# Sixteen of the first layer's 24 stored tiles keep two short first steps, the last eight take one long first step

## The chip, the core and the metric

The program runs on one core of a Trainium2 chip. The engines that matter here are PE (TensorE, matrix products), DVE (VectorE), ACT (ScalarE) and SP, whose queue issues the loads from memory. The metric is the device time of one execution in microseconds (us).

## What is computed

One block of a network over 256 tokens and 2048 features, in float32. A vector `c` gives nine modulation vectors of 2048; then come a gated feed-forward layer, a mixer and a second feed-forward layer. The change lies in the first feed-forward layer.

```python
mod = (jax.nn.silu(c) @ w_ada[l] + b_ada[l]).reshape(B, N_SUBLAYERS, N_MOD, D_MODEL)
def swiglu(h, w_gate, w_up, w_down):
    return (jax.nn.silu(h @ w_gate) * (h @ w_up)) @ w_down
h = modulate(rms_norm(x, gain_pre), shift, scale)     # shift, scale: two of the nine
y = rms_norm(fn(h), gain_post)
return x + weight * (1 + gate[:, None, :]) * y
```

`w_gate` and `w_up` are 2048 x 5632, `w_ada` is 2048 x 18432.

## The kernel before, in words

The 2048 features are 16 blocks of 128. `h` can be made for a feature block only when its columns of `w_ada` (all 2048 rows of them) have been read and summed. So the layer begins by rounds over feature blocks, FIRST_BLOCKS (line 27): round 0 takes blocks 0 and 1, round 1 blocks 2 and 3, and rounds 2, 3 and 4 four blocks each. While one round multiplies, the columns of `w_ada` for a later one are read.

Method `outer` (line 667) runs the rounds. At the start of one, `block` makes `h` for its blocks (`hT` in the rows): products of `x` with a diagonal (`mm<-scale,x`), two ACT passes and one DVE subtraction per block. Then the round goes through 14 loads, numbered 0 to 13 here, gate and up in turn. A load is 512 columns of a weight matrix, that is four tiles of 128 columns, over the feature blocks of the round: 512 KB for two blocks, 1 MB for four. For each two blocks of it, ACT rounds the weights to `hi` (line 186), DVE takes the rest as `lo` (line 187), and PE runs 24 products of 128x256 (line 202: for each tile and block hi with both halves of `h`, then lo with the first).

Loads 0 and 1 keep their sums in PSUM over all rounds. Loads 2 to 13 cannot: these are the 24 stored tiles (FF_SPILL1; a tile is 128 columns of both gate and up). Their products of one step are taken out of two PSUM banks into SBUF tiles `act`: the first step is copied by ACT (line 704), every later one is added by DVE (line 706). MERGES1 (line 28) says at the end of which round a stored load makes a step and from which block: in the first layer at the end of every round. MERGES2, for the second layer, leaves out the end of round 0 and lets the step after round 1 take blocks 0 to 3 in one go.

After each load's issue, `tick` (line 1471) advances the sums over `w_ada` by a number of ticks that RATES (line 30) sets by round: 1.0 per load in round 0, 1.25 in rounds 1 to 3. A tick (`ada_long`) issues one 512 KB piece of `w_ada` (two DMAs of 256 KB) and lets DVE multiply and add the piece of three ticks before (lines 277 and 279: two operations 512 wide for the pieces of round 1, one 1024 wide for later ones). The modulation for round 1 takes 14 ticks: eight pieces, three ticks of lag, three of hold; the last step are products with ones on PE (`mm<-ones,acc`) and a bias by DVE (`mod`).

What sets the order: a scheduler fixes, when the program is built, the order of the instructions on each engine; each engine then runs its list in that order. Loads and pieces of `w_ada` go through SP's one queue in program order. A weight load (`raw`) has four buffers, a piece (`ada`) four, `hi` and `lo` four each, and PSUM eight banks, four of them held by loads 0 and 1. A piece waits at SP for the DVE sum that frees its buffer, and everything behind it in SP's queue waits with it.

Of the kernel before, what the change touches and what calls it, by code (L numbers as in the profile page):

```python
# [17 lines left out]
P = 128  # L18
# [4 lines left out]
EPS = 1e-6  # L23
LN_EPS = 1e-5 * 64
FF_OUTER = 4
FF_SPILL1, FF_SPILL2 = 24, 16
FIRST_BLOCKS = ((0, 2), (2, 2), (4, 4), (8, 4), (12, 4))
MERGES1 = {2: 0, 4: 2, 8: 4, 12: 8, 16: 12}
MERGES2 = {4: 0, 8: 4, 12: 8, 16: 12}
RATES = (1.0, 1.25, 1.25, 1.25, 0.9)  # L30
GROUPS1, GROUPS2 = (28, 16), (20, 16, 8)
ADA_AHEAD = ((7, 6), 2)
ADA_FFN1, ADA_END, ADA_FFN2 = 1.5, 1.5, 0.34
# [49 lines left out]
class Block:  # L83
# [580 lines left out]
            with self.tc.high_priority() if apart else nullcontext():  # L664
                done(*part, banks[b][:, :part[2]])

    def outer(self, blocks, loads, block, tick, piece, merges=None):

        nc = self.nc
        for q, (b0, bn) in enumerate(blocks):
            block(b0, bn)
            for i, (w, c0, n, outs, parts) in enumerate(loads):
                k0, kn = b0, bn
                if parts is not None:
                    if b0 + bn not in merges:
                        tick(q, i)  # L680
                        continue
                    k0 = merges[b0 + bn]
                    kn = b0 + bn - k0
                raw = self.load(w, k0, kn, c0, n)
                tick(q, i)
                nk = min(kn, (512 if self.gates else piece) // n)
                row, t0, t1 = outs, 0, KD - 1
                if parts is not None:
                    banks = [outs() for _ in parts]
                    row = [((2 * b + j) * P, bank[:, j, :], j == 0, j == 1) for b, bank in enumerate(banks)  # L690
                           for j in range(2)]
                    t0, t1 = k0, k0 + kn - 1
                for pc in range(0, kn, nk):
                    hi, lo = self.split(raw[:, pc:pc + nk, :])
                    for off, ps, first, last in row:
                        for k in range(nk):
                            kt = k0 + pc + k
                            cs = slice(off, off + P)
                            self.mm3(ps, hi[:, k, cs], lo[:, k, cs], self.hT[:, kt],
                                     first and kt == t0, last and kt == t1)  # L700
                if parts is not None:
                    for part, bank in zip(parts, banks):
                        if k0 == 0:
                            nc.scalar.copy(part, bank)  # L704
                        else:
                            nc.vector.tensor_tensor(part, part, bank, ALU.add)  # L706

    def ffn(self, wg, wu, wd, every, ada, mm, actp, blocks, merges, block, outer_tick, first, spill, spare, groups, post_begin, post_done, ahead, late=0):
        nc = self.nc
        chunk = 0  # L710
        last = None
# [1 line left out]
        bank = lambda: self.tile(mm, [P, 2, T], tag="mm")  # L713
# [35 lines left out]
        loads = []  # L749
# [6 lines left out]
        for i in range(0, len(spilled), 2):  # L756
            for which, w in enumerate((wg, wu)):
                parts = [a[:, :, which, :] for a in spilled[i:i + 2]]
                loads.append((w, (first + 2 * i) * P, 2 * P * len(parts), bank, parts))
        self.outer(blocks, loads, block, outer_tick, 1024, merges)  # L760
        for i, (gate, up) in enumerate(zip(*pss)):
            act(gate, up, spare > i)
        for a in spilled:
# [2 lines left out]
        for gi, n in enumerate(groups):  # L766
# [24 lines left out]
            for cb in range(4):  # L791
                apart = final and cb == 3
                banks = [self.tile(mm, [P, 512], tag="mm") for _ in range(3 if apart else 2)]
# [55 lines left out]
    def mixer(self, ctx):  # L849
# [72 lines left out]
        def stage(a, b, b_old, pieces, rate, tasks={}):  # L922

            nonlocal ends
            for s in range(SLOTS):
                for _ in range(int((s + 1) * rate) - int(s * rate)):
                    next(pieces, None)
                for run, at in ((b_old, range(SLOTS)), (b, range(SLOTS)), (a, A_SLOTS)):
                    if run and s in at:
                        next(run, None)  # L930
                if s in tasks:
                    tasks[s]()
                if s in ADA_SLOTS[not a] and (s in MOD_SLOTS[not a] or not ends):
                    ends = next(ada, None)
# [520 lines left out]
    def run(self):  # L1455
        I = self.I
        self.constants()
        with ExitStack() as ph:
            mm, actp = self.ffn_pools(ph, False, 12)
            self.begin(mm)  # L1460
            accs = cycle((lambda: self.tile(self.accs, [P, 4 * T], tag="acc"),
                          lambda: self.tile(self.raws, [P, 4 * T], tag="acc", bufs=1)))
            ada = self.ada_long((5,), 3, 3, accs, lambda: self.tile(mm, [P, 512], tag="mm"))

            def block(k0, n):
                q = [b[0] for b in FIRST_BLOCKS].index(k0)
                while self.ada_pos < self.ada_end[(1, 0), q]:
                    next(ada)
                self.pre_block(0, k0, n, mm)

            def tick(q, i):
                if q == len(FIRST_BLOCKS) - 1 and i == 0:
                    self.begin_rest(mm)
                for _ in range(int((i + 1) * RATES[q]) - int(i * RATES[q])):
                    next(ada, None)

            self.ffn(I["ffn1_w_gate"], I["ffn1_w_up"], I["ffn1_w_down"], ADA_FFN1, lambda: next(ada, None), mm, actp,
                     FIRST_BLOCKS, MERGES1, block, tick, FF_OUTER, FF_SPILL1, (FF_SPILL1 + FF_OUTER) // 2 - 12, GROUPS1,
                     lambda *a: self.post_begin(0, 0.5, True, mm, *a), lambda tt: None, True, ADA_END)
            for _ in ada:  # L1480
                pass
        with ExitStack() as ph:
            self.phase(ph, 2, 0, 2, 300)
            self.mixer(ph)
        with ExitStack() as ph:
            mm, actp = self.ffn_pools(ph, True, 8)
            bank = lambda: self.tile(mm, [P, 512], tag="mm")
            ada = self.ada_run((8,), lambda n: self.tile(self.raws, [P, 4 * T], tag="ada", bufs=self.ada_bufs), 3, bank)

            def block(k0, n):  # L1490
                while self.ada_pos < self.ada_end[(7, 6), [b[0] for b in FIRST_BLOCKS].index(k0)]:
                    next(ada)
                self.next_block(2, k0, n, mm)

            def tick(q, i):
                for _ in range((i < 2 if q < 2 else 2 - i % 2) if q < 4 else 0):
                    next(ada, None)

            self.ffn(I["ffn2_w_gate"], I["ffn2_w_up"], I["ffn2_w_down"], ADA_FFN2, lambda: next(ada, None), mm, actp,
                     FIRST_BLOCKS, MERGES2, block, tick, FF_OUTER, FF_SPILL2, (FF_SPILL2 + FF_OUTER) // 2 - 8, GROUPS2,  # L1500
                     lambda *a: (list(ada), self.post_begin(2, 0.5, False, mm, *a)),
                     self.store, False)

# [26 lines left out]
```

## Time and profile before

| what | value |
|---|---|
| median of three runs | 2107.4 us (2106.2 to 2109.78) |
| the profiled execution | 2101.59 us |
| its span on the core | 2099.7 us |
| PE busy | 2054.2 us, 98% |
| DVE busy | 1597.6 us, 76% |

How to read it: the span is cut by the rounds. Round 0 multiplies from about 29 to 72.6 us of the span, round 1 from 72.6 to 125.4, round 2 to 204, round 3 to 290. A row of the timeline gives the start, the duration, the engine, the line and what is written from what; in brackets stand the idle time before it and who ended that.

### The profile page before, as it was taken

What the parts mean: (1) busy time and instruction counts of PE and PEld (TensorE: products, weight loads), DVE (VectorE), ACT (ScalarE), POOL (GpSimd) and SP (SyncE); (2) the same over time, 40 slices, a digit from 0 to 9 for tenths busy, and PEclk for the clock granted to TensorE, in tenths of its full rate; (3) what the DMA queues carried; (4) which work ended last, traced back from release to release, by engine and by line L of the source; (5) the groups of instructions that cost most, each with busy time, mean ns of one, the idle gap of its engine ahead of it and who ended that gap; (6) DMA issues with size and microseconds to landing.
All of it is one profiled execution on the core that took longest, in us unless ns stands there. A gap on an engine that the chain in (4) does not pass through costs nothing. (4 is left out here: it accounts for less than half of the span.)

```text
span 2099.7 us, 39553 instructions
## 1 busy us (share of the span) xinstructions
PE 2054.2 (98%) x16395; PEld 1831.4 (87%) x16395; DVE 1597.6 (76%) x2213; ACT 1010.3 (48%) x1475; POOL 0.2 (0%) x4
## 2 busy tenths in 40 slices
PE   7899999999999999999999999999999999999998
PEld 5899999888888888899898977899998888888886
DVE  4899899887888976687888955867899655555556
ACT  4443345433444545655555644554364344443453
POOL 0000000000000000000000000000000000000000
PEclk9999999999999999999999999999999999999999
DMA  9999887799999955665555444686988756555553
GB/s 336 310 339 342 309 306 274 283 326 323 321 326 330 351 178 172 182 195 146 162 146 165 131 166 141 241 303 232 328 283 296 258 186 192 190 182 199 190 191 120
DMA packets 307761, 506.66 MB, mean 241 GB/s; under 512 B 13205, under 2 KB 157694, under 8 KB 307070
## 3 DMA queue, kind: packets, MB, share of 16 engines
q1 hardware_dynamic: 306092, 500.78, 70.2%
q10 hardware_dynamic: 1490, 3.36, 0.5%
q8 instruction: 128, 2.10, 0.4%
q14 instruction: 51, 0.42, 0.1%
HBM read 499.87 MB, written 4.22 MB: 240 GB/s over the span
## 5 line engine op out<-in xcount | busy, mean ns | idle before, releaser
L186 ACT CAST hi<-raw 128x1024 fp32r<-128x1024 f32 (+2 forms) x762 | 692.9, 915 | 870.9 <-PE mm L202 558.2
L187 DVE TENSOR_TENSOR lo<-raw,hi 128x1024 fp32r<-128x1024 f32 (+2 forms) x762 | 796.6, 1052 | 361.7 <-ACT hi L186 356.3
L202 PE MATMUL mm<-hT,hi 128*128 128x256 f32 x4160 | 755.0, 284 | 9.1 <-DVE hT L463 4.4
L202 PEld LDWEIGHTS mm<-hT,hi 128*128 128x128 f32 x4160 | 637.9, 188 | 25.6 <-issue 7.2
L202 PE MATMUL mm<-hT,lo 128*128 128x256 f32 x2080 | 579.4, 280 | 6.4 <-DVE lo L187 6.4
L213 PE MATMUL mm<-hT,hi 128*128 128x512 f32 x1280 | 448.5, 394 | 0.0
L202 PE MATMUL mm<-hi,act 128*128 128x512 f32 (+1 forms) x1328 | 399.5, 382 | 0.0
L202 PEld LDWEIGHTS mm<-hT,lo 128*128 128x128 f32 x2080 | 391.1, 189 | 7.7 <-DVE lo L187 7.6
L214 PE MATMUL mm<-hT,lo 128*128 128x256 f32 x1280 | 359.2, 281 | 0.0
L279 DVE SCALAR_TENSOR_TENSOR acc<-ada,csilu,acc 128x1024 f32<-128x1024 f32 (+1 forms) x240 | 298.9, 1246 | 48.0 <-DMA ada<-in_w_ada_dram 46.8
L213 PEld LDWEIGHTS mm<-hT,hi 128*128 128x128 f32 x1280 | 240.7, 188 | 56.0
L202 PEld LDWEIGHTS mm<-hi,act 128*128 128x128 f32 x1328 | 246.4, 188 | 48.1
L202 PE MATMUL mm<-lo,act 128*128 128x512 f32 (+1 forms) x664 | 253.3, 381 | 0.0
L214 PEld LDWEIGHTS mm<-hT,lo 128*128 128x128 f32 x1280 | 239.8, 187 | 0.1
L202 PEld LDWEIGHTS mm<-lo,act 128*128 128x128 f32 x664 | 124.8, 188 | 24.0
L706 DVE TENSOR_TENSOR act<-act,mm 128x512 f32<-128x512 f32 x144 | 96.0, 679 | 1.7 <-PE mm L202 1.3
L279 DVE SCALAR_TENSOR_TENSOR ada<-x,csilu,ada 128x512 f32<-128x512 f32 (+1 forms) x45 | 41.2, 916 | 0.1
L202 PE MATMUL mm<-hi,work 128*128 128x512 f32 x128 | 41.0, 391 | 0.0
L458 ACT ACTIVATE hT<-mm,mod,gs 128x256 fp32r<-128x256 f32 x48 | 27.1, 569 | 14.4 <-PE mm L202 14.4
L704 ACT COPY act<-mm 128x512 f32<-128x512 f32 x40 | 23.4, 586 | 18.5 <-PE mm L202 18.0
L741 ACT ACTIVATE silu<-silu 128x512 f32<-128x512 f32 x20 | 12.6, 632 | 33.2 <-DVE silu L740 33.0
L202 PEld LDWEIGHTS mm<-hi,work 128*128 128x128 f32 x128 | 24.0, 188 | 5.0
(413 smaller groups left out, 1655.8 us busy)
## 6 DMA issues: line engine op xcount, KB each, us to landing
raw<-in_ffn_w_down_dram SPq DMA_DIRECT2D x88, 1024.0 KB
raw<-in_ffn_w_gate_dram SPq DMA_DIRECT2D x80, 1024.0 KB
raw<-in_ffn_w_up_dram SPq DMA_DIRECT2D x80, 1024.0 KB
ada<-in_w_ada_dram SPq DMA_DIRECT2D x160, 512.0 KB
ada<-in_w_ada_dram SPq DMA_DIRECT2D x192, 256.0 KB
raw<-in_w_in_dram SPq DMA_DIRECT2D x34, 1024.0 KB
x<-in_w_ada_dram SPq DMA_DIRECT2D x64, 256.0 KB
raw<-in_w_out_dram SPq DMA_DIRECT2D x16, 1024.0 KB
```

The lines of the kernel that those rows point to most:

```text
L186: a = nc.scalar.copy(hi, raw)
L187: d = nc.vector.tensor_tensor(lo, raw, hi.bitcast(F32), ALU.subtract)
L202: return self.pe(self.nc.tensor.matmul(ps, a, b, start=start, stop=stop))
L213: nc.tensor.matmul(ps.rearrange("p a t -> p (a t)"), hi, x.rearrange("p a t -> p (a t)"), start=start, stop=False)
L214: nc.tensor.matmul(ps[:, 0, :], lo, x[:, 0, :], start=False, stop=stop)
L279: self.later(nc.vector.scalar_tensor_tensor(acc, raw[:, i], ck, acc, ALU.mult, ALU.add))
L458: a = nc.scalar.activation(self.hT[:, k, 0, :], ps[:, j, :], AF.Identity, scale=g, bias=sh)
L704: nc.scalar.copy(part, bank)
L706: nc.vector.tensor_tensor(part, part, bank, ALU.add)
L741: last = nc.scalar.activation(s, s, AF.Silu)
```

## The change

FF_EARLY1 = 16: the stored loads 2 to 9 (16 tiles) go on by MERGES1, now FROM_TWO. Loads 10 to 13 (eight tiles) go by the other table, now FROM_FOUR: nothing in round 0, and in round 1 one load of 1 MB over blocks 0 to 3. The second layer has FF_EARLY2 = 0, as before all by FROM_FOUR. In round 0 the rate is 1.4 and ticks are taken at loads 0 to 9 only, 14 as before.

```diff
-FF_SPILL1, FF_SPILL2 = 24, 16
+FF_SPILL1, FF_SPILL2, FF_EARLY1, FF_EARLY2 = 24, 16, 16, 0
-MERGES1 = {2: 0, 4: 2, 8: 4, 12: 8, 16: 12}
-MERGES2 = {4: 0, 8: 4, 12: 8, 16: 12}
-RATES = (1.0, 1.25, 1.25, 1.25, 0.9)
+FROM_TWO, FROM_FOUR = {2: 0, 4: 2, 8: 4, 12: 8, 16: 12}, {4: 0, 8: 4, 12: 8, 16: 12}
+RATES = (1.4, 1.25, 1.25, 1.25, 0.9)
...
-                    if b0 + bn not in merges:
+                    if b0 + bn not in parts[1]:
...
-                    k0 = merges[b0 + bn]
+                    k0 = parts[1][b0 + bn]
...
-                loads.append((w, (first + 2 * i) * P, 2 * P * len(parts), bank, parts))
+                loads.append((w, (first + 2 * i) * P, 2 * P * len(parts), bank,
+                              (parts, FROM_TWO if 2 * i < early else FROM_FOUR)))
...
-                for _ in range(int((i + 1) * RATES[q]) - int(i * RATES[q])):
-                    next(ada, None)
+                if q or i < 10:
+                    for _ in range(int((i + 1) * RATES[q]) - int(i * RATES[q])):
+                        next(ada, None)
```

Where instructions move. First ACT in round 0, about load 5. Before, the rounding of load 5 stands right behind the copies of load 3's two banks (`mm_339`, `mm_340`):

```order
L704 COPY act_202<-mm_339 128x2x256
L704 COPY act_203<-mm_340 128x2x256
L186 CAST hi_419<-raw_410 128x1024
L704 COPY act_204<-mm_378 128x2x256
L704 COPY act_205<-mm_379 128x2x256
```

After, load 3's banks are `mm_344` and `mm_345`, load 4's `mm_388` and `mm_389`, and load 5 is `raw_420`:

```order
L703 COPY act_202<-mm_344 128x2x256
L703 COPY act_203<-mm_345 128x2x256
L703 COPY act_204<-mm_388 128x2x256
L185 CAST hi_429<-raw_420 128x1024
L703 COPY act_205<-mm_389 128x2x256
```

The rounding of load 5 now stands behind the copy of load 4's first bank, one copy later. The same has moved at load 8.

Second, ACT at the end of round 0. Before, the rounding of round 1's first load (`raw_780`) stands behind the copies of load 12's banks, ahead of both copies of the last load, 13 (`mm_734`, `mm_735`):

```order
L704 COPY act_212<-mm_689 128x2x256
L704 COPY act_213<-mm_690 128x2x256
L186 CAST hi_786<-raw_780 128x1024
L704 COPY act_212<-mm_734 128x2x256
L704 COPY act_213<-mm_735 128x2x256
L458 ACTIVATE hT_94<-mm_769,mod_105,gs_766 128x256
```

After, the last load of the round is load 9 (`mm_598`, `mm_599`), the one ahead of it load 8 (`mm_549`, `mm_550`), and round 1's first is `raw_644`:

```order
L703 COPY act_208<-mm_549 128x2x256
L703 COPY act_209<-mm_550 128x2x256
L703 COPY act_208<-mm_598 128x2x256
L185 CAST hi_650<-raw_644 128x1024
L703 COPY act_209<-mm_599 128x2x256
L457 ACTIVATE hT_94<-mm_633,mod_105,gs_630 128x256
```

The rounding for round 1 now waits for the last load's first bank. On DVE the `lo` of that load and one `w_ada` sum stand ahead of the `hT` subtraction in both orders.

Third, DVE in round 1, from load 8 to load 10. Before (`raw_1084`, `raw_1122` and `raw_1160` are loads 8, 9 and 10):

```order
L187 TENSOR_TENSOR lo_1093<-raw_1084,hi_1092 128x1024
L279 SCALAR_TENSOR_TENSOR acc_646<-ada_1049,csilu_95,acc_646 128x1024
L187 TENSOR_TENSOR lo_1131<-raw_1122,hi_1130 128x1024
L706 TENSOR_TENSOR act_208<-act_208,mm_1090 128x2x256
L706 TENSOR_TENSOR act_209<-act_209,mm_1091 128x2x256
L187 TENSOR_TENSOR lo_1169<-raw_1160,hi_1168 128x1024
```

After (`raw_948`, `raw_986` and `raw_1024`):

```order
L186 TENSOR_TENSOR lo_957<-raw_948,hi_956 128x1024
L278 SCALAR_TENSOR_TENSOR acc_544<-ada_913,csilu_95,acc_544 128x1024
L186 TENSOR_TENSOR lo_995<-raw_986,hi_994 128x1024
L705 TENSOR_TENSOR act_208<-act_208,mm_954 128x2x256
L705 TENSOR_TENSOR act_209<-act_209,mm_955 128x2x256
L276 TENSOR_SCALAR acc_1092<-ada_951,csilu_95 128x1024
L705 TENSOR_TENSOR act_208<-act_208,mm_992 128x2x256
L278 SCALAR_TENSOR_TENSOR acc_1092<-ada_989,csilu_95,acc_1092 128x1024
L705 TENSOR_TENSOR act_209<-act_209,mm_993 128x2x256
L186 TENSOR_TENSOR lo_1033<-raw_1024,hi_1032 128x1024
```

Two sums and load 9's two additions now stand ahead of load 10's `lo`.

## Rows read from the trace of the kernel before

**Rows 1.** Busy time of each engine in stretches of the span, with the number of instructions in brackets, then the granted PE clock, the share of the DMA engines and GB/s. The stretches are round 0, round 1, its two parts, and round 2.
```profile
29.00:72.60 43.60, 43.13 (x352) 42.82 (x352) 35.19 (x40) 28.18 (x42) 0.00 (x0) 0.96 1.02 351
72.60:125.40 52.80, 45.60 (x374) 43.66 (x372) 49.06 (x60) 20.85 (x28) 0.00 (x0) 1.00 0.87 294
72.60:84.00 11.40, 10.29 (x84) 9.79 (x83) 9.40 (x11) 6.95 (x10) 0.00 (x0) 1.00 0.93 307
84.00:125.40 41.40, 35.31 (x293) 33.87 (x291) 39.66 (x50) 13.90 (x19) 0.00 (x0) 1.00 0.86 290
125.40:204.00 78.60, 78.43 (x666) 78.43 (x667) 73.26 (x78) 29.87 (x30) 0.00 (x0) 1.00 0.97 348
```

**Rows 2.** Timeline of PE from 64 to 126 us, only its waits and the products with ones and with the diagonal.
```profile
65.62 0.95 PE L202 MATMUL mm<-ones,acc 128*128 128x1 f32 x8
...
72.14 0.61 PE L202 MATMUL mm<-scale,x 128*128 128x128 f32 x4
73.45 0.50 PE L202 MATMUL mm<-hT,hi 128*128 128x256 f32 x2 [0.70 <-ACT hT L458]
74.36 0.38 PE L202 MATMUL mm<-hT,hi 128*128 128x256 f32 x1 [0.41 <-DVE hT L463]
...
88.21 0.39 PE L202 MATMUL mm<-hT,lo 128*128 128x256 f32 x1 [1.83 <-DVE lo L187]
95.58 0.38 PE L202 MATMUL mm<-hT,lo 128*128 128x256 f32 x1 [0.63 <-DVE lo L187]
102.63 0.38 PE L202 MATMUL mm<-hT,lo 128*128 128x256 f32 x1 [1.80 <-DVE lo L187]
110.95 1.95 PE L202 MATMUL mm<-ones,acc 128*128 128x1 f32 x16
116.33 0.39 PE L202 MATMUL mm<-hT,lo 128*128 128x256 f32 x1 [0.50 <-DVE lo L187]
119.16 1.05 PE L202 MATMUL mm<-scale,x 128*128 128x128 f32 x8
122.41 1.05 PE L202 MATMUL mm<-scale,x 128*128 128x128 f32 x8
125.57 0.39 PE L202 MATMUL mm<-hT,lo 128*128 128x256 f32 x1 [1.44 <-DVE lo L187]
```

**Rows 3.** Timeline of PE in round 0: the first products of load 8 and of load 9, and what follows each.
```profile
53.84 0.63 PE L202 MATMUL mm<-hT,hi 128*128 128x256 f32 x4
54.31 0.28 PE L202 MATMUL mm<-hT,lo 128*128 128x256 f32 x1
...
56.67 0.63 PE L202 MATMUL mm<-hT,hi 128*128 128x256 f32 x4
57.14 0.28 PE L202 MATMUL mm<-hT,lo 128*128 128x256 f32 x1
```

**Rows 4.** Timeline of ACT in the same stretch: the rounding of load 9, the copies of load 8's two banks, the rounding of load 10; then the two passes over a feature block that make `h` at the start of round 2.
```profile
54.53 1.05 ACT L186 CAST hi<-raw 128x1024 fp32r<-128x1024 f32 x1
55.69 0.59 ACT L704 COPY act<-mm 128x512 f32<-128x512 f32 x1
56.87 0.59 ACT L704 COPY act<-mm 128x512 f32<-128x512 f32 x1 [0.59 <-PE mm L202]
57.35 1.05 ACT L186 CAST hi<-raw 128x1024 fp32r<-128x1024 f32 x1
...
121.98 0.56 ACT L458 ACTIVATE hT<-mm,mod,gs 128x256 fp32r<-128x256 f32 x1
122.44 0.55 ACT L462 ACTIVATE work<-mm,mod,gs 128x256 f32<-128x256 f32 x1
```

**Rows 5.** Timeline of DVE: a piece for round 1 (two operations) and the `lo` behind it; the `lo` of load 10 in round 0; the `hT` subtraction of round 1; and, from 101.36, the `lo` of load 8 in round 1 and what follows.
```profile
34.38 1.53 DVE L279 SCALAR_TENSOR_TENSOR acc<-ada,csilu,acc 128x512 f32<-128x512 f32 x2
35.82 1.22 DVE L187 TENSOR_TENSOR lo<-raw,hi 128x1024 fp32r<-128x1024 f32 x1
...
58.44 1.23 DVE L187 TENSOR_TENSOR lo<-raw,hi 128x1024 fp32r<-128x1024 f32 x1 [0.41 <-ACT hi L186]
...
73.88 0.42 DVE L463 TENSOR_TENSOR hT<-work,hT 128x256 fp32r<-128x256 f32 x1 [0.82 <-ACT work L462]
...
101.36 1.21 DVE L187 TENSOR_TENSOR lo<-raw,hi 128x1024 fp32r<-128x1024 f32 x1
102.50 1.27 DVE L279 SCALAR_TENSOR_TENSOR acc<-ada,csilu,acc 128x1024 f32<-128x1024 f32 x1
103.70 1.21 DVE L187 TENSOR_TENSOR lo<-raw,hi 128x1024 fp32r<-128x1024 f32 x1
104.83 1.27 DVE L706 TENSOR_TENSOR act<-act,mm 128x512 f32<-128x512 f32 x2
106.03 1.21 DVE L187 TENSOR_TENSOR lo<-raw,hi 128x1024 fp32r<-128x1024 f32 x1
107.16 0.68 DVE L706 TENSOR_TENSOR act<-act,mm 128x512 f32<-128x512 f32 x1
107.76 0.74 DVE L277 TENSOR_SCALAR acc<-ada,csilu 128x1024 f32<-128x1024 f32 x1
108.42 0.68 DVE L706 TENSOR_TENSOR act<-act,mm 128x512 f32<-128x512 f32 x1
```

**Rows 6.** Timelines of SP and ACT: the issue of a 512 KB load and of a 1 MB load, each followed by the rounding that waited for it.
```profile
73.99 0.38 SPq L176 DMA_DIRECT2D raw<-in_ffn_w_gate_dram  x1
...
79.71 1.06 ACT L186 CAST hi<-raw 128x1024 fp32r<-128x1024 f32 x1 [2.11 <-DMA raw<-in_ffn_w_gate_dram]
...
119.00 0.39 SPq L176 DMA_DIRECT2D raw<-in_ffn_w_up_dram  x1
...
127.37 2.00 ACT L186 CAST hi<-raw 128x1024 fp32r<-128x1024 f32 x2 [1.64 <-DMA raw<-in_ffn_w_up_dram]
```

**Rows 7.** What SP's queue waited for from 29 to 126 us: total, times, longest (us).
```profile
SPq L269 <- DVE acc L279: 38.1, 26, 3.6
SPq L176 <- DVE lo L187: 10.6, 13, 1.9
```

**Rows 8.** Timeline of PE at the starts of rounds 3 and 4: the waits for `hT`.
```profile
209.62 0.38 PE L202 MATMUL mm<-hT,hi 128*128 128x256 f32 x1 [1.03 <-DVE hT L463]
...
293.13 0.39 PE L202 MATMUL mm<-hT,hi 128*128 128x256 f32 x1 [0.51 <-DVE hT L463]
```

More of the change, by code (lines that the diff above doesn't have):

```diff
@@ L665, in rows_block, with outer @@
                 done(*part, banks[b][:, :part[2]])
-    def outer(self, blocks, loads, block, tick, piece, merges=None):
+    def outer(self, blocks, loads, block, tick, piece):
         nc = self.nc
@@ L688, in outer @@
                 if parts is not None:
-                    banks = [outs() for _ in parts]
+                    banks = [outs() for _ in parts[0]]
                     row = [((2 * b + j) * P, bank[:, j, :], j == 0, j == 1) for b, bank in enumerate(banks)
@@ L701, in outer @@
                 if parts is not None:
-                    for part, bank in zip(parts, banks):
+                    for part, bank in zip(parts[0], banks):
                         if k0 == 0:
@@ L706, in outer, with ffn @@
                             nc.vector.tensor_tensor(part, part, bank, ALU.add)
-    def ffn(self, wg, wu, wd, every, ada, mm, actp, blocks, merges, block, outer_tick, first, spill, spare, groups, post_begin, post_done, ahead, late=0):
+    def ffn(self, wg, wu, wd, every, ada, mm, actp, blocks, early, block, outer_tick, first, spill, spare, groups, post_begin, post_done, ahead, late=0):
         nc = self.nc
@@ L758, in ffn @@
                 parts = [a[:, :, which, :] for a in spilled[i:i + 2]]
-                loads.append((w, (first + 2 * i) * P, 2 * P * len(parts), bank, parts))
-        self.outer(blocks, loads, block, outer_tick, 1024, merges)
+                loads.append((w, (first + 2 * i) * P, 2 * P * len(parts), bank,
+                              (parts, FROM_TWO if 2 * i < early else FROM_FOUR)))
+        self.outer(blocks, loads, block, outer_tick, 1024)
         for i, (gate, up) in enumerate(zip(*pss)):
@@ L1473, in tick @@
                     self.begin_rest(mm)
-                for _ in range(int((i + 1) * RATES[q]) - int(i * RATES[q])):
-                    next(ada, None)
+                if q or i < 10:
+                    for _ in range(int((i + 1) * RATES[q]) - int(i * RATES[q])):
+                        next(ada, None)
             self.ffn(I["ffn1_w_gate"], I["ffn1_w_up"], I["ffn1_w_down"], ADA_FFN1, lambda: next(ada, None), mm, actp,
-                     FIRST_BLOCKS, MERGES1, block, tick, FF_OUTER, FF_SPILL1, (FF_SPILL1 + FF_OUTER) // 2 - 12, GROUPS1,
+                     FIRST_BLOCKS, FF_EARLY1, block, tick, FF_OUTER, FF_SPILL1, (FF_SPILL1 + FF_OUTER) // 2 - 12, GROUPS1,
                      lambda *a: self.post_begin(0, 0.5, True, mm, *a), lambda tt: None, True, ADA_END)
@@ L1499, in run @@
             self.ffn(I["ffn2_w_gate"], I["ffn2_w_up"], I["ffn2_w_down"], ADA_FFN2, lambda: next(ada, None), mm, actp,
-                     FIRST_BLOCKS, MERGES2, block, tick, FF_OUTER, FF_SPILL2, (FF_SPILL2 + FF_OUTER) // 2 - 8, GROUPS2,
+                     FIRST_BLOCKS, FF_EARLY2, block, tick, FF_OUTER, FF_SPILL2, (FF_SPILL2 + FF_OUTER) // 2 - 8, GROUPS2,
                      lambda *a: (list(ada), self.post_begin(2, 0.5, False, mm, *a)),
```

## The prediction

> **What bounds the kernel now.** I read the table of stretches first. In round 0 PE is busy 43.13 of 43.60 us, although DMA moves 351 GB/s; from 125.40 on it is busy 78.43 of 78.60 us [rows 1]. Only round 1 has room: 45.60 busy of 52.80 us, 7.2 us idle, and there DVE is busy 39.66 of the 41.40 us from 84 on [rows 1]. Next, PE's waits by name: in round 1 the long ones are for `lo` from DVE, 1.83, 0.63, 1.80 and 0.50 us, and one of 1.44 us at the start of round 2 [rows 2]. Third, what makes DVE late. SP's queue stood 38.1 us in 26 waits for sums over `w_ada` [rows 7], so loads arrive just in time, but with DVE 96% busy (39.66 / 41.40) the loop of sum, freed buffer, next load runs at DVE's pace. So PE is the bound where its lists are fed in time, DVE in round 1, and what counts is the sum of PE's waits up to round 2. Behind that PE is full, so a shift at round 2's start should reach the end one to one.
>
> **Prices from the rows.** A load of 512 KB takes PE 56.67 - 53.84 = 2.83 us for 24 products, 0.118 us each; its first four need `hi` alone, 54.31 - 53.84 = 0.47 us [rows 3]. On DVE, start to start: a sum 103.70 - 102.50 = 1.20 us, a `lo` 104.83 - 103.70 = 1.13, two additions 106.03 - 104.83 = 1.20, a first sum 108.42 - 107.76 = 0.66 us [rows 5]. On ACT, a copy 57.35 - 56.87 = 0.48 and a rounding 1.05 us; the copy of a load's first bank starts 55.69 - 53.84 = 1.85 us after the load's first product [rows 3, 4].
>
> **What is removed and moved without cost.** Four loads of two blocks go from round 0 to round 1: 4 x 24 x 0.118 = 11.3 us of PE work earlier out, later in, sum nothing. Roundings, `lo`s, copies, bytes and ticks keep their counts. Gone are eight DVE additions, 8 x 0.60 = 4.8 us. But which ones? Loads 2 to 9 keep theirs. Between load 8's `lo` at 102.63 and load 12's at 116.33 PE needs 4 x 2.83 + 1.95 (16 products with ones) = 13.3 us and takes 13.7 [rows 2, 3]. So the additions of loads 10 to 13 were taken where PE hardly waited, while the stretch up to load 8 (28.3 us from 74.36 to 102.63, against 8 x 2.83 + 0.47 = 23.1 of work [rows 2, 3]) has the same DVE list in both orders: its 5 us of waits stay. That is why I do not book the 4.8 us.
>
> The Trainium skill (Perfetto Trace Analysis, section Identifying the Most-Contended Engine) says to find the engine with the most occupancy and to optimize it first, and its next section allows for that engine to change between regimes. By the first sentence alone DVE's saving would count whole in round 1; rows 2 deny it for the place where the additions go. It returns as a rival.
>
> **Round 0, the casts.** The rounding of load 5 now stands behind the copy of load 4's first bank: counted from load 4's first product it starts at 1.85 + 0.48 = 2.33 and ends at 3.38 us, while PE is free at 2.83. The `lo` takes 0.04 + 1.23 us more (58.44 against the rounding's end at 58.40 [rows 4, 5]), to 4.65; PE, without waits, would want it at 2.83 + 0.47 = 3.30. Price 1.35 us. Load 8 has the same place, but between its first four products and the `lo`s stand the products with ones, 0.95 us [rows 2]: there 3.38 - 2.83 = 0.55 us. Either can cost from 0 to a whole load, 2.83 us; a gain is excluded, since PE never waited in round 0's middle.
>
> **Round 0 to 1.** From the first product of load 9: first half of the diagonal products 0.61 [rows 2], first bank's copy at 2.46, rounding 2.94 to 3.99, `lo` to 5.26 less the overlap, a sum, 6.4, and `hT` of 0.42 us [rows 5] until 6.8. PE ends its products at 2.83 + 2 x 0.61 = 4.05. Before, PE resumed at 74.36, 1.61 us after its diagonal products ended at 72.75; now 2.8, so 1.2 us more. Bounds: -0.4 (the wait of 0.41 us at 74.36 gone) to 2.8.
>
> Ticks are denser: 14 over ten loads. A piece for round 1 costs DVE 35.82 - 34.38 = 1.44 us [rows 5], so a load costs it 1.13 + 1.4 x 1.44 = 3.15 us at first and 1.13 + 1.4 x 1.20 = 2.8 with the later pieces, PE 2.83. DVE stood idle 43.60 - 35.19 = 8.4 us in round 0 [rows 1], which hides the eight pieces' excess of some 0.3 us a load. I book nothing beyond the three waits; what the denser pieces ask of the transfers is a rival below.
>
> **Round 1, load 10.** From the end of load 8's `lo`, DVE's list is: sum 1.20, `lo` 1.13, two additions 1.20, first sum 0.66, addition 0.60, sum 1.20, addition 0.60, `lo` 1.21: 7.8 us [rows 5]. PE has 20 + 24 + 4 products until it needs it, 48 x 0.118 = 5.7 us. A new wait of 2.1 us; bounds 0, if DVE catches up, and 4.8, what the additions were worth. Behind it a load of four blocks is 5.66 us of PE against 2 x 1.13 + 1.25 x 1.20 = 3.8 of DVE: no wait, and DVE gets ahead. So the waits of 0.50 and 1.44 us [rows 2] go, -1.94.
>
> The 1 MB loads must land whole before their first rounding. A 512 KB load took 79.71 - 73.99 = 5.7 us from issue to rounding, a 1 MB load 127.37 - 119.00 = 8.4 [rows 6], 2.7 more. Load 10 is issued behind two pieces freed by sums that end before load 8's additions, some 10 us ahead of its place in DVE's list (my estimate from the order and the prices above); 8.4 + 1.05 fit, by a hair. If uncovered: up to 2.7 us more.
>
> The Trainium skill (Perfetto Trace Analysis, section DMA Optimizations) says that splitting a DMA lets parts start sooner, and speaks against this merging; its point on larger DMAs speaks for it. By the first the sum would be 2.7 us higher, by rows 6 with the cover nothing; by the second it would fall only if transfers set round 1's pace, and DMA is at 0.86 there [rows 1].
>
> **Start of round 2.** The 16 diagonal products, 2 x 1.05 us [rows 2], now follow the last product of the round instead of standing among them, so less covers `hT`: 1.05 + 1.01 (two ACT passes, 122.44 + 0.55 - 121.98 [rows 4]) + 0.42 [rows 5] + hand-overs of 0.3, a guess, = 2.8 against 2.1 + 0.47: 0.2 us, between 0 and 1.03, what round 3's start shows [rows 8].
>
> **Sum.** 1.35 + 0.55 + 1.2 + 2.1 + 0.2 - 1.94 = 3.5 us slower. Against the profiled execution, 2101.59 us (span 2099.7 and 1.9 around it), that is 2105.1. That execution is 5.8 us under the median of the runs, 2107.4; on the median I predict 2110.9 us. Its own range, with some of the bounds hit together, is 2107.5 to 2114.5.
>
> **Rivals.** First, *DVE's relief counts*: round 0 has enough slack for the moved casts, and the 4.8 us fall out of round 1. For it: DVE at 96% there. Against it: the additions went from where PE did not wait. 2107.4 - 4.8 = 2102.6 us. This is the result by the skill's rule on the most-contended engine, named above.
>
> Second, *the transfers set round 0's pace*, slower: a load and 1.4 ticks are 0.524 + 0.734 = 1.26 MB, at 351 GB/s [rows 1] 3.6 us against 2.83; over ten loads 7.5 us more, in place of the casts' 3.1. It decides once the four buffers ahead are used up and SP's queue cannot refill them. For it: DMA share 1.02 in round 0. Against it: the loads needed first are issued before the round, and SP waited for DVE, not for DMA [rows 7]. 2107.4 + 7.5 + 0.4 = 2115.3 us.
>
> Third, *a shift and nothing else*: the moved copies come early enough on the chip, PE stays full in round 0, and only round 1's own terms (2.1 + 0.2 - 1.94) are left: 2107.8 us. For it: the waits of 1.03 and 0.51 us at rounds 3 and 4 [rows 8] may also shrink with DVE ahead.
>
> **Chances.** My forecast 0.45, the first rival 0.20, the second 0.13, the third 0.22. What a measurement of this kernel can tell from no change is about 0.2%, 4.2 us. My case is over that in about four of ten (0.19), the second rival nearly always: slower 0.33. The first rival is under -4.2 us in six of ten, and the others seldom: faster 0.17. Within: 0.50. The range from 2103.5 to 2115.5 leaves out half of the first rival and half of the second, 0.17.
>
> **What would show it.** In the profile after: waits of PE for the rounding and the `lo` of load 5, about 1.3 us some 15 us into round 0, and at load 8; the first `hT` wait near 2 us instead of 0.41; round 1's start near 64 us of the span, not 72.6; waits for `lo` at loads 4, 6 and 8 as before; a new one near 2 us at load 10 and none behind it; round 2's start near 128.5 us, not 125. Round 0 without PE waits would make my first three terms wrong; waits for DMA at ACT's roundings in round 0 would speak for the second rival; a round 1 whose early waits shrink would speak for the first.

## The result and the profile after

The changed kernel takes 2113.34 us in the median of ten runs (2110.48 to 2121.47), the kernel before, timed beside it, 2105.79 us in the median of ten (2101.87 to 2109.78). The medians differ by 7.5 us; the ratio of the runs is 1.0042, with a 95% interval from 1.0030 to 1.0054. The prediction said 3.5 us slower.

| what | after |
|---|---|
| the profiled execution | 2110.48 us |
| its span | 2108.7 us |
| PE busy | 2058.8 us, 98% |
| DVE busy | 1591.5 us, 75% |

DVE is busy 6.1 us less than before, PE does the same work, and the span is 9.0 us longer. The table of stretches, cut at the rounds as in [rows 1] (round 0, round 1, and the like part of round 2; two lines of 2 us are set between):

```profile
29.00:62.40 33.40, 31.65 (x251) 30.89 (x251) 28.61 (x34) 18.47 (x27) 0.00 (x0) 0.95 1.00 349
62.40:131.00 68.60, 59.78 (x470) 58.20 (x468) 56.77 (x61) 28.34 (x36) 0.00 (x0) 0.95 0.95 340
66.00:68.00 2.00, 2.00 (x12) 2.00 (x12) 1.84 (x3) 1.16 (x2) 0.00 (x0) 0.60 1.05 392
68.00:70.00 2.00, 2.00 (x12) 2.00 (x11) 2.00 (x3) 1.04 (x1) 0.00 (x0) 0.55 1.05 385
131.00:209.00 78.00, 76.38 (x667) 76.16 (x667) 68.73 (x76) 31.02 (x35) 0.00 (x0) 1.00 0.86 302
```

PE is idle 1.75 us in round 0 and 8.8 us in round 1, before 0.47 and 7.2. New is the third number from the end, the granted clock: 0.60 and 0.55 from 66 to 70 us, means over its two levels (0.50 is 1.2 GHz, 1.00 is 2.4 GHz). PE's timeline shows the waits ahead of that fall, and answers to [rows 2]:

```profile
45.33 0.73 PE L201 MATMUL mm<-hT,hi 128*128 128x256 f32 x4 [0.44 <-ACT hi L185]
46.59 0.38 PE L201 MATMUL mm<-hT,lo 128*128 128x256 f32 x1 [0.53 <-DVE lo L186]
55.31 0.74 PE L201 MATMUL mm<-hT,hi 128*128 128x256 f32 x4 [0.45 <-ACT hi L185]
...
63.96 0.50 PE L201 MATMUL mm<-hT,hi 128*128 128x256 f32 x2 [0.95 <-ACT hT L457]
65.80 0.39 PE L201 MATMUL mm<-hT,hi 128*128 128x256 f32 x1 [1.33 <-DVE hT L462]
81.34 0.39 PE L201 MATMUL mm<-hT,lo 128*128 128x256 f32 x1 [2.21 <-DVE lo L186]
88.71 0.38 PE L201 MATMUL mm<-hT,lo 128*128 128x256 f32 x1 [0.63 <-DVE lo L186]
95.77 0.39 PE L201 MATMUL mm<-hT,lo 128*128 128x256 f32 x1 [1.80 <-DVE lo L186]
105.05 0.39 PE L201 MATMUL mm<-hT,lo 128*128 128x256 f32 x1 [1.83 <-DVE lo L186]
...
129.08 1.95 PE L201 MATMUL mm<-scale,x 128*128 128x128 f32 x16
131.35 0.74 PE L201 MATMUL mm<-hT,hi 128*128 128x256 f32 x4 [0.33 <-ACT hT L457]
133.38 0.39 PE L201 MATMUL mm<-hT,hi 128*128 128x256 f32 x1 [1.29 <-DVE hT L462]
```

The reader sees the forecast's waits at their places: load 5 and load 8 of round 0, `hT` at the start of round 1 (behind its two waits the clock falls in this execution), loads 4, 6 and 8 as before, a new one at load 10 and none behind it. Last comes one that was forecast at 0.2 us, and here is 0.33 + 1.29. What makes load 5 late is seen on ACT: the copy of load 4's first bank waits for PE, and the rounding starts behind it, as the change's order has it.

```profile
43.75 0.59 ACT L703 COPY act<-mm 128x512 f32<-128x512 f32 x1 [1.06 <-PE mm L201]
44.23 1.05 ACT L185 CAST hi<-raw 128x1024 fp32r<-128x1024 f32 x1
45.18 0.59 ACT L703 COPY act<-mm 128x512 f32<-128x512 f32 x1
45.65 1.06 ACT L185 CAST hi<-raw 128x1024 fp32r<-128x1024 f32 x1
```

It does not end there. Round 3's diagonal products start at 211.62 us, before at 206.14. Round 4's start at 294.88, before at 290.18. But the mixer's first product (`sa<-hT,hi`) starts at 810.12, before at 801.87: between round 4 and the mixer, where the change touches nothing, another 3.6 us are lost. Table of stretches from 300 to 780 us, then PE's waits there, of after:

```profile
300.00:780.00 480.00, 477.17 (x2689) 414.04 (x2688) 408.16 (x441) 219.16 (x265) 0.00 (x0) 1.00 0.86 305
```

```profile
306.05 0.29 PE L144 MATMUL mm<-consts,work 115*128 115x115 f32 x1 [0.45 <-DMA work<-in_lnx_b_dram]
...
577.56 0.38 PE L213 MATMUL mm<-hT,lo 128*128 128x256 f32 x1 [1.20 <-DVE lo L186]
...
745.47 0.50 PE L201 MATMUL mm<-lo,act 128*128 128x512 f32 x1 [1.09 <-DVE lo L186]
```

The kernel before has no wait there at all, 480.00 busy of 480.00 us:

```profile
300.00:780.00 480.00, 480.00 (x2702) 417.11 (x2701) 418.67 (x462) 226.40 (x275) 0.00 (x0) 1.00 0.87 307
```

What DVE does ahead of the wait at 745 us, timeline of DVE, after:

```profile
738.04 1.29 DVE L278 SCALAR_TENSOR_TENSOR acc<-ada,csilu,acc 128x1024 f32<-128x1024 f32 x1 [5.55 <-DMA ada<-in_w_ada_dram]
739.25 0.68 DVE L806 TENSOR_TENSOR act<-y,mm 128x512 f32<-128x512 f32 x1
739.85 1.22 DVE L186 TENSOR_TENSOR lo<-raw,hi 128x1024 fp32r<-128x1024 f32 x1
...
744.21 3.48 DVE L186 TENSOR_TENSOR lo<-raw,hi 128x1024 fp32r<-128x1024 f32 x3
```

A sum over `w_ada` stood 5.55 us for its piece, and the `lo` that PE wants came behind it. The lists of instructions show why this stretch can differ though the change is far away: the scheduler sets up the whole program anew, and DVE's, ACT's and SP's lists of before and after are the same again, word for word, only from about 760 us on.

So two questions: what made the early loss (to round 3), and what made the late one (round 4 to the mixer).

### The profile page after: what moved, and what is told of

Its sections match the earlier page's. It is cut to its first block, busy times and chain, and to the rows that moved or that the text cites. A ratio compares the mean times of both kernels' runs of the same rounds, so it can differ in the third digit from the quotient of the medians.

```text
span 2108.7 us, 39528 instructions
## 1 busy us (share of the span) xinstructions
PE 2058.8 (98%) x16395; PEld 1834.5 (87%) x16395; DVE 1591.5 (75%) x2205; ACT 1006.8 (48%) x1475; POOL 0.2 (0%) x4
## 5 line engine op out<-in xcount | busy, mean ns | idle before, releaser
L705 DVE TENSOR_TENSOR act<-act,mm 128x512 f32<-128x512 f32 x136 | 91.1, 683 | 5.2 <-PE mm L201 4.7
```

## The experiments

For each execution two stretches are read from PE's timeline: *early*, from the first diagonal products of round 0 to the first of round 3, and *late*, from the first of round 4 to the mixer's first product. The runs stand in the order in which they were made; the table of all is at the end of the section. Where no ratio stands, a run is a single execution.

**The roundings back in their place.** In round 0 a bank's copy waits in ACT's list for the next load's rounding.

```diff
+                    for part, bank in held:
+                        self.after(nc.scalar.copy(part, bank), self.cast, "order")
...
-                        if k0 == 0:
+                        if k0 == 0 and q == 0 and not self.gates and len(loads) == 14:
+                            held.append((part, bank))
```

> The changed kernel with one thing undone: in round 0 the rounding of the next load stands ahead of both copies of a load, as in the kernel before; the copies come later. If the moved roundings are what round 0 lost: PE's waits at loads 5 and 8 of round 0 (0.44 + 0.53 and 0.45 us) go, the waits for hT at the start of round 1 (0.95 + 1.33 us) fall to about 1.1, the granted clock stays at 1.00 from 66 to 70 us (0.55 to 0.60 in the changed kernel), and round 3's diagonal products start at 207.5 to 209.5 us instead of 211.6. If the denser ticks over w_ada were the cause and the roundings only stood there: within 1 us of 211.6.

Measured: 2111.58 us, round 3 at 213.37; neither number of the expectation. Of the waits, load 5 keeps one of 0.92 us for `lo`, load 8 none, the `hT` waits are 0.65, 0.41 and 0.56, and the granted clock is 1.00 throughout round 1. From round 0's diagonal products to round 2's this run takes 98.57 us, the change 102.33: the moved roundings and the clock behind them are worth 3.8 us (3.2 against the second trace of the change, which takes 101.77). They are gone again by round 3 (early 184.96 against 184.87), because round 2 took 86.39 us here and 82.54 there. Of these 3.9 us 2.3 are PE's pace, see the last section; from 125 to 204 us the granted clock was 0.98, as it stood at 0.50 from 132.0 to 135.4 us.

**The wait filled.** Five useless products stand in the wait at the start of round 1, so that PE is not idle.

```diff
+            if s == 0 and k0 == 2:
+                fill = self.tile(psum, [P, 512], tag="mm")
+                for _ in range(5):
+                    nc.tensor.matmul(fill, self.scale[:, 0, :], self.x[:, 0, :512], start=True, stop=True)
```

> The changed kernel with five idle products of 512 columns on PE behind the diagonal products of round 1, so that PE works while it waits for hT. If the fall of the granted clock after that wait costs time of its own: the clock stays near 1.00 from 66 to 70 us, the wait for lo at load 4 (81.34 us) ends 1.0 to 1.7 us earlier and round 3 starts at 210 to 210.6. If DVE sets the pace there anyway, or the clock falls for another reason: load 4 and round 3 (211.6) move by less than 0.5 us.

```profile
66.00:70.00 4.00, 4.00 (x23) 2.80 (x22) 3.84 (x6) 3.02 (x4) 0.00 (x0) 1.00 1.04 384
```

Measured: the clock stays at 1.00 where it had been 0.60 and 0.55, load 4 waits 0.43 instead of 2.21 us, and round 3 starts at 210.67. That the filler held the clock up is not shown by this one execution: the second trace of the changed kernel, below, has the same two waits and the clock at 1.00 behind them as well. The fillers themselves ran 4.46 us and overran the wait, so early, 184.33 us, is 0.5 us under the changed kernel's first trace and equal to its second. The execution took 2104.04 us, which looked like a gain; it was timed later.

**No late additions.** In the kernel before, the eight additions of loads 10 to 13 in round 1 are left out (the output lacks those products).

```diff
-                        else:
+                        elif not (len(loads) == 14 and q == 1 and i >= 10):
```

> The kernel before with the additions of loads 10 to 13 in round 1 left out (eight of them; their sums are then wrong). If these additions were taken where PE hardly waited: round 3's diagonal products start 0 to 1.9 us earlier than 206.1. If every DVE operation saved in round 1 counts: 4.8 us earlier, 201.3.

```profile
86.81 0.39 PE L202 MATMUL mm<-hT,lo 128*128 128x256 f32 x1 [1.83 <-DVE lo L187]
94.18 0.38 PE L202 MATMUL mm<-hT,lo 128*128 128x256 f32 x1 [0.63 <-DVE lo L187]
101.24 0.39 PE L202 MATMUL mm<-hT,lo 128*128 128x256 f32 x1 [1.80 <-DVE lo L187]
...
124.11 1.22 PE L202 MATMUL mm<-hT,hi 128*128 128x256 f32 x4 [2.19 <-ACT hi L186]
126.88 0.58 PE L202 MATMUL mm<-hT,lo 128*128 128x256 f32 x1 [1.55 <-DVE lo L187]
```

Measured: round 3 at 209.15, early 183.42: 4.6 us *longer* than before, outside both expectations. The waits at loads 4, 6 and 8 are those of [rows 2] to 0.03 us, so taking away 4.8 us of DVE's work at loads 10 to 13 bought nothing. The freed places were filled by other instructions, round 2's first rounding came late (2.19 and 1.55 us), and the clock was 0.65 and 0.78 in the 12 us from 122. The late stretch is 511.74 us, as before; more on that below.

**No early additions.** The same with the eight additions of loads 2 to 5 left out.

```diff
-                        else:
+                        elif not (len(loads) == 14 and q == 1 and 2 <= i < 6):
```

> The kernel before with the additions of loads 2 to 5 in round 1 left out (eight of them; their sums are then wrong). If DVE is the bound up to load 8: PE's waits at loads 4 to 8 shrink and round 3 starts 3 to 5 us earlier than 206.1. If the arrival of the loads sets the pace there: less than 1 us earlier.

Measured: the waits at loads 4 and 6 are gone, and others stand further back: 0.27, 2.22, 1.45 and 0.88 us from 97 to 118 us and 1.33 for `hT`. Early is 181.51, 2.7 us longer than before, again outside both expectations. DVE's work in round 1 was cut at one place and at another, and neither cut brought round 3 nearer. In both runs the clock fell behind a wait (here from 118.4 to 121.8 us), so part of the longer way is the clock's.

**Both kernels once more,** unchanged, each for a second trace.

> The changed kernel once more, to see which of its waits come back. First theory (what the order fixes comes back): the same waits of PE within 0.1 us, that is 0.44 and 0.53 at load 5, 0.45 at load 8, 0.95 and 1.33 for hT at the start of round 1, 1.83 at load 10, 1.29 for hT at round 2, and later 0.45 near 306, 1.20 near 577 and 1.09 us near 745 us; the diagonal products of round 3 start 211.6 us into the span and the span is 2108.7, both within 0.5. Rival (the waits behind round 2 and the pace of PE fall by chance in each execution): the early waits come back, but the waits near 306, 577 and 745 differ by more than 0.3 us each, and the span differs by 2 us or more.

> The kernel before once more. First theory: round 3's diagonal products start 206.1 us into the span, no wait of PE over 0.3 us between 300 and 780 us, span 2099.7 within 0.5. Rival (chance): waits of 0.5 us or more turn up between 300 and 780 us, or the stretches in which PE's 256 wide products follow each other at 113 instead of 118 ns lie elsewhere, and the span differs by 2 us or more.

Stretches of the changed kernel's second trace:

```profile
66.00:68.00 2.00, 0.51 (x2) 0.30 (x2) 2.00 (x4) 2.00 (x5) 0.00 (x0) 1.00 1.05 394
68.00:70.00 2.00, 1.87 (x15) 1.87 (x16) 1.83 (x4) 1.50 (x2) 0.00 (x0) 1.00 1.04 388
104.00:106.00 2.00, 1.91 (x10) 1.92 (x11) 2.00 (x3) 1.22 (x2) 0.00 (x0) 0.58 1.05 389
```

Measured: spans of 2115.3 and 2100.8 us. Of the changed kernel all early waits come back (0.45 and 0.52, 0.44, 0.95 and 1.33, then 2.21, 0.63, 1.61, 1.51, 0.32 and 1.29), the clock falls at another place (0.58 and 0.57 from 104 to 108 us, and 1.00 from 66 to 70), and early is 184.31. At the start of round 0 it was 0.50 from 33 to 36 us, where the first trace has 0.97 from 32 to 36: that, too, differs by execution, and round 0 took 34.05 us here and 32.85 there. The late waits do not come back as they were: 0.72 at 306.9, 0.83 at 464.4, 0.41, 0.31, 1.27 at 556.2, 0.53 and 2.88 us at 746.6, in all 7.1 us of idle PE from 300 to 780. Late is 520.11, 4.9 us longer than in the first execution. The kernel before repeats both stretches to 0.4 us, again without a wait from 300 to 780. So the early loss is 5.1 to 6.0 us in these traces and its waits sit in the lists; the late one, 3.6 and 8.4 us, is there each time and differs in size.

**The ticks alone.** All 24 tiles make their first step in round 0, and the ticks are the change's.

```diff
-FF_SPILL1, FF_SPILL2, FF_EARLY1, FF_EARLY2 = 24, 16, 16, 0
+FF_SPILL1, FF_SPILL2, FF_EARLY1, FF_EARLY2 = 24, 16, 24, 0
```

> Only the ticks of round 0: 1.4 for each of loads 0 to 9, none at 10 to 13; all 24 tiles make their first step in round 0, as before. If the late roundings come from the denser ticks alone: waits of 0.9 to 1.0 us at load 5 and 0.45 at load 8 in round 0, none at load 10 in round 1, and the diagonal products of round 3 1.0 to 2.5 us later than before. If they come from the loads that left round 0: no waits in round 0 and round 3 within 0.5 us of before. Whole time 1 to 5 us over before by the first, within 1 us by the second; a time at or over that of the changed kernel (+7.5) would say that the ticks are the loss.

```profile
84.00:116.00 32.00, 31.62 (x269) 31.42 (x268) 30.01 (x38) 9.47 (x9) 0.00 (x0) 1.00 0.87 302
```

```profile
306.22 0.43 PE L144 MATMUL mm<-consts,work 115*128 115x115 f32 x1 [5.05 <-DMA ada<-in_w_ada_dram]
```

Measured: ratio 1.0074 (1.0045 to 1.0103), 2117.83 us in the median, 4.5 us over the whole change's, though the two intervals overlap. By the total the ticks would be the loss. The trace denies it for the early part: the late roundings are there (0.44 and 0.52, 0.45, and once more 0.45 and 0.52 at load 11), but with the sums done earlier the waits at loads 4, 6 and 8 are gone. From 84 to 116 us PE is busy 31.62 of 32.00 us; in the kernel before, 27.51. Early is 179.22, as before. All of the loss is late, 526.50, with one wait of 5.05 us near 306 us, behind which the granted clock is 0.50 to 310 us.

**The loads alone.** Loads 10 to 13 leave round 0, ticks stay at one for each of 14 places.

```diff
-RATES = (1.4, 1.25, 1.25, 1.25, 0.9)
+RATES = (1.0, 1.25, 1.25, 1.25, 0.9)
...
-                if q or i < 10:
+                if True:
```

> Only the loads: loads 10 to 13 leave round 0 as in the change, and the ticks stay at one for each of 14 places, so the last four fall together behind load 9. No waits of PE at loads 5 and 8 in round 0; three sums ahead of the subtraction for hT, so a wait of 1 to 2 us there; 1.83 at load 10, about 1.3 for hT at round 2. If the moved roundings and the wait they made were the early loss: round 3's diagonal products 1 to 2.5 us later than before, and the whole 1 to 4 us slower. If the loads that left round 0 are the loss whatever the ticks: round 3 at 5 us or more later, the whole 6 us or more.

```profile
65.52 1.23 PE L201 MATMUL mm<-hT,hi 128*128 128x256 f32 x4 [3.72 <-ACT hi L185]
```

```profile
64.00:70.00 6.00, 4.45 (x19) 4.16 (x20) 5.14 (x6) 2.09 (x2) 0.00 (x0) 0.50 1.03 376
```

Measured: ratio 1.0060 (1.0038 to 1.0082), round 3 at 214.00, early 186.27. No wait in the middle of round 0, but 3.72 us at the start of round 1, where the first rounding now stands behind `hT`, and PE at 0.50 of its clock behind it. Set beside the ticks alone: the denser ticks cost nothing early (+0.4 and 0.0 us against the two traces of before), the loads that left round 0 cost 7.0 to 7.4. The change with both seems to lie between, at 5.1 to 6.0, but its two traces have PE's quick pace in round 2 (last section), worth 2.3 us, and the loads alone, the ticks alone and the kernel before have the slow one. With the slow pace the changed kernel's early lists took 187.40 us (sums behind `lo`, below), 8.2 to 8.5 more than before: the denser ticks did not make the loads' loss smaller. My reading of why the loads cost so much, argued from the lists and not shown by a run of its own: with the ticks done by load 9, loads 10 to 13 are the time in which DVE gets ahead of PE before `hT` must be made, and the change takes just these loads out.

**One useless product, and two,** in the kernel *before*, at the start of round 2. Nothing of the change is in them.

```diff
+            if s == 0 and k0 == 4 and i == 2:
+                fill = self.tile(psum, [P, 512], tag="mm")
+                for _ in range(1):
+                    nc.tensor.matmul(fill, self.scale[:, 0, :], self.x[:, 0, :512], start=True, stop=True)
```

> The kernel before with one useless product of 512 columns in float32 (two passes, 0.45 us each in the earlier run that used five) on PE at the start of round 2. The lists of ACT and SP stay word for word, DVE's changes in two places near round 2. Both theories: up to 0.9 us later from round 2 on, no new wait of PE between 300 and 780 us, DVE's waits there for pieces of w_ada 28 to 35 us in sum as in the two executions of before, the whole 0 to 1.5 us slower. This is the control for the run with two.

> The same with two useless products, 1.8 us, which is enough for the scheduler to set up the lists of DVE, ACT and SP anew from round 2 to about 760 us. Theory that the lists set up anew are the late loss: DVE waits 45 us or more for pieces of w_ada between 290 and 780 us, PE gets new waits of 2 us or more in sum there for lo or for the small loads near 306 us, and the whole is 3 to 10 us slower, though nothing of the change is in it. Rival, that the late loss belongs to the change (its loads, its ticks or its shift of 5 us): DVE's waits for pieces stay near 30 us, no new wait of PE, and the whole is 0.5 to 2.5 us slower.

Table of stretches from 300 to 780 us of the run with one, then of the run with two; then PE's wait near 306 us of the latter:

```profile
300.00:780.00 480.00, 480.00 (x2720) 416.98 (x2719) 418.87 (x462) 226.12 (x276) 0.00 (x0) 1.00 0.86 307
```

```profile
300.00:780.00 480.00, 475.89 (x2673) 411.64 (x2672) 409.73 (x444) 221.16 (x266) 0.00 (x0) 1.00 0.86 306
```

```profile
304.59 0.42 PE L145 MATMUL mm<-consts,work 115*128 115x115 f32 x1 [2.61 <-DMA ada<-in_w_ada_dram]
```

Measured: with one, ratio 0.9989 (0.9973 to 1.0004), no difference. With two, 1.0043 (1.0027 to 1.0060): the same loss as the change's, from 1.8 us of useless work of which early shows nothing (178.56). PE is idle 4.1 us from 300 to 780 and late is 516.77. In its trace another 6 us came behind the mixer's start, where its lists are before's word for word: 1294.6 us to the start of PE's last product, 1284.3 to 1290.5 in the traces of all other kernels but the next. That part is the execution's, not the list's: the clock fell three times there (0.57 from 809 to 813 us, 0.57 from 833 to 837, 0.50 from 878 to 881), where before's trace has no fall. One expectation failed: DVE waited 45.3 us for pieces in the run with one, not 28 to 35, and PE lost nothing by it, so that sum alone does not tell a good list from a bad one.

**Sums behind `lo`.** In the changed kernel, from round 4 on, no sum over `w_ada` stands on DVE ahead of the `lo` of an earlier load.

```diff
+        if self.after_rounds:
+            self.after(op, self.last_lo, "order")
```

> The changed kernel, where from round 4 on no sum over w_ada may stand on DVE ahead of the lo of a load issued before it. If sums that stand too early and wait for their piece are what makes PE wait late: PE's waits for lo between 300 and 780 us fall from 2.3 and 6.2 us (the two executions of the changed kernel) to under 1 us, and the whole is 2 to 5 us faster than the changed kernel, 2108 to 2111. Rival, that the pieces themselves come late whatever the place of the sums: DVE's waits for pieces keep over 45 us, PE's waits for lo stay at 2 us or more, and the time stays at 2113 or over.

Measured: 2120.44 us in the median, ratio 1.0079 (1.0052 to 1.0106). No sum waits for a piece from 290 to 780 us any more. But now DVE stands 53.1 us there for roundings, SP 272.0 us for sums that must free a buffer, PE still waits for `lo`, 1.68 us at 386.6 and 2.17 at 745.8, and late is 516.57. Both theories of that expectation fall: the sums' place is not the whole cause, since without those waits the loop of sum, buffer, load makes others.

**The filled wait, timed.**

> The changed kernel with five useless products in PE's first wait of round 1, as in e2_fill_wait, now timed. There one execution took 2104.04 us, under all ten of the changed kernel (2110.48 to 2121.47), while DVE's list is the changed kernel's from round 1 on, and ACT's and SP's throughout. If the filler is worth what that one execution showed (PE's clock held up behind the wait, and pieces that land in time later): a median of 2102 to 2108 us, ratio to before up to 1.002. If that execution was a lucky one of lists that are set: a median of 2110 to 2116 us, as the changed kernel, and the late waits are the lists' alone.

Measured: 2114.46 us in the median of six, ratio 1.0057 (1.0038 to 1.0076). The 2104.04 us were one lucky execution of the same lists. Early is 183.44, late 519.27 (in the lucky one 514.80), and from the mixer's first product to the start of PE's last one it is 1289.0 us (in the lucky one 1284.3). The clock is 1.00 from 66 to 70 us in both filled executions, and behind the unfilled waits it fell in two of three (changed kernel's first trace, sums behind `lo`): the wait leaves room for the fall but does not fix it.

All executions with a trace, in us:

| kernel | early | late |
|---|---|---|
| before; again | 178.86; 179.23 | 511.69; 511.73 |
| one useless product in before | 179.74 | 509.85 |
| before without late additions | 183.42 | 511.74 |
| changed; again | 184.87; 184.31 | 515.24; 520.11 |
| changed, roundings back | 184.96 | 516.44 |
| changed, wait filled; again | 184.33; 183.44 | 514.80; 519.27 |
| changed, sums behind `lo` | 187.40 | 516.57 |
| loads alone | 186.27 | 515.85 |
| ticks alone | 179.22 | 526.50 |
| before without early additions | 181.51 | 520.94 |
| two useless products in before | 178.56 | 516.77 |

The late column parts into two. The first three lines (four executions, 509.85 to 511.74) are the kernels whose lists of DVE, ACT and SP are before's throughout the late stretch, and PE is idle in none of them from 300 to 780. In the other ten (514.80 to 526.50) the scheduler has set these lists up anew, whatever the edit was, and each has 2.8 to 8.8 us of idle PE there. That it is the list and not the delay shows in two runs. The one without late additions comes 3.0 us late to round 4 (293.20 against 290.18), with before's lists from about 270 us on, and loses nothing more; the ticks alone come 0.3 us late (290.52), with new lists, and lose most. Differences between the ten mean less: the changed kernel, roundings back, wait filled and loads alone have the same late lists word for word, and their six executions range from 514.80 to 520.11. In the early column the quick pace of round 2 is in three figures, both of the changed kernel and the first of the wait filled.

## Why the prediction was right, and where not

Sign and range held; the size, 3.5 us against 7.5, was low. That the median still fell within the range is in part luck: the range was made of the bounds of the early terms, and two larger things had no term, the late loss and PE's quick pace in round 2, which hid 2.3 us in both traces of the changed kernel. By its steps:

- *Casts of loads 5 and 8:* 1.35 and 0.55 us forecast, 0.97 and 0.45 measured, in both traces.
- *Round 0 to 1:* 1.2 us over before. Measured 0.95 + 1.33 against 0.70 + 0.41: 1.17 more.
- *Waits at loads 4, 6 and 8 stay:* 2.21, 0.63, 1.80 us against 1.83, 0.63, 1.80. *Load 10:* 2.1 forecast, 1.83 and 1.51 measured. *Nothing behind it:* so it is.
- *Start of round 2:* 0.2 forecast, 1.62 measured. The term counted the two ACT passes and the subtraction and left out what stands ahead of them in the lists: on ACT a copy, and on DVE a sum of 1.28 us that started at 131.71, the subtractions only at 132.91. The 1.03 us of [rows 8] were no upper bound. With what was measured the forecast's own terms add up to 0.97 + 0.45 + 1.17 + 0.38 + 1.83 + 1.62 - 1.94 = 4.5 us.
- *The clock* had no term. In the first trace it fell to 0.60 and 0.55 behind the `hT` waits, 2 x 0.40 + 2 x 0.45 = 1.7 us, and to 0.71 from 95 to 100 us, 5 x 0.29 = 1.5 us more; in the second it fell once in round 1, from 104 to 108 us.
- *"Behind that PE is full, so a shift at round 2's start should reach the end one to one"* is the step that failed. The shift reached round 4 as +4.7 us and the mixer as +8.2. PE is full there only with before's lists. The prediction read the moved places of the lists near the change and took the rest for unchanged.

The rivals: DVE's relief, the result by the rule of the Trainium skill (Perfetto Trace Analysis, section Identifying the Most-Contended Engine) that the most occupied engine is optimized first, did not come; the traces disagree with it here, since without the late additions the waits at loads 4 to 8 were the same three (1.83, 0.63, 1.80). Transfers did not set round 0's pace: ACT's roundings there wait for a load once, 2.23 us at 33.99 us (0.79 at 33.08 before; 2.27 at 35.11 with the ticks alone), no wait of PE follows, and at loads 5 and 8 the roundings are late behind copies that wait for PE. The shift alone was too small.

What stays open: which place in the new lists makes the late waits. Two hints, a sum that waits 5.55 us and small loads that come late near 306 us, are each only part of it. A changed early part with before's late lists was not tried, as the scheduler sets the lists. No version here beats the kernel before.

## What to carry to other kernels

Where a scheduler sets up the whole program anew, compare the lists of instructions to the end, not only around the edit, and make a control run in which nothing of the change is moved: two useless products cost here as much as the change. Read the same kernel's trace twice before a wait of a microsecond is explained. And when work is taken out of a stage that ends in a hand-over, ask who used that stage to get ahead.

## What was not expected of the hardware

PE's products 256 wide follow each other at one of two paces with the granted clock at 1.00, and the same lists give either. Timeline of PE in round 2 of the filled wait, first execution, then second:

```profile
149.98 0.28 PE L201 MATMUL mm<-hT,lo 128*128 128x256 f32 x1
150.10 0.39 PE L201 MATMUL mm<-hT,hi 128*128 128x256 f32 x2
150.32 0.28 PE L201 MATMUL mm<-hT,lo 128*128 128x256 f32 x1
```

```profile
149.78 0.28 PE L201 MATMUL mm<-hT,lo 128*128 128x256 f32 x1
149.90 0.40 PE L201 MATMUL mm<-hT,hi 128*128 128x256 f32 x2
150.13 0.28 PE L201 MATMUL mm<-hT,lo 128*128 128x256 f32 x1
```

Three products take 0.34 us in the first, 0.35 in the second; on the mean from 140 to 190 us 113.3 and 117.8 ns each. Between the diagonal products of rounds 2 and 3 that is 82.55 and 84.87 us. The changed kernel had the quick pace in round 2 in both traces, a gift of 2.3 us that hid part of its early loss; what chooses the pace no run here shows.
